# Five edits of a two-layer encoder trunk: unit setting, conv taps, V of the meta rows, input rows, last FFN part

## The chip, the cores and the metric

The kernel runs on one core of a Trainium2 chip. A core has TensorE (PE) for matrix products, VectorE (DVE), ScalarE (ACT) and GpSimd (POOL) for work on rows and elements, and SyncE (SP), which here starts most of the transfers. Each engine works through its own instructions in their order; semaphores tie the engines together. The metric is the device time of one execution in microseconds (us); the median of three runs of the kernel before is 1964.85.

## The reference, cut to what matters

The input is 512 tokens of width 1024; 16 learned meta rows are put in front, so 528 rows go through. A layer norm comes first, then two layers of the same form.

```
h = concatenate([meta, x]); h = layer_norm(h, ln_in_g, ln_in_b)
for l in range(2):
    h = layer_norm(ALPHA * h + 0.5 * swiglu_ffn(h, ffn1_w13[l], ffn1_w2[l]), ...)
    z = h @ w_in[l]                       # xp, ca, cg, q, k, v, g
    y_pool = trailing means of xp over 2, 4, 8, 16 rows, minus xp, times a matrix
    y_conv = silu(layer_norm(depthwise conv of ca * sigmoid(cg), 31 taps)) @ w_pw
    y_ret  = retention, 4 heads: rope(q), rope(k), chunk-causal decay, v, norm, silu gate
    h = layer_norm(ALPHA * h + concatenate([y_pool, y_conv, y_ret]) @ w_out[l], ...)
    h = layer_norm(ALPHA * h + 0.5 * swiglu_ffn(h, ffn2_w13[l], ffn2_w2[l]), ...)
return h[16:]
```

## The kernel before, in words

The activations lie with features on the 128 partitions and rows along the free dimension, in two halves of 264 rows (256 tokens and 8 meta rows). A product in float32 accuracy is made of three matmuls on rounded parts: high by high, high by low, low by high. The high part of a weight tile is a ScalarE cast, the low part a VectorE subtraction (`weights`, L86 to L95). Weight tiles rotate through small pools: 4 raw ones, 5 high and 5 low ones. Another pool, `wide`, has 16 tiles of 128 x 558 for rows of the mixers and for some splits. PSUM has four banks with the tag `acc`, two `att`, two `stat`.

The stages are the input (to about 66 us), an FFN, the mixer `m0` (about 366 to 610), two FFNs, the mixer `m1` (about 1335 to 1575), and the last FFN `f1b` (`last_ffn`), whose output leaves as rows of tokens.

A mixer computes the gated conv input u (two tiles `m1u`) and xp (`m1xp`), then V (L664 to L693): for each of four token tiles (`tt` 0 to 3) and the 16 meta rows (`tt` 4) a product of 24 matmuls of 512 columns, its means per head (VectorE, L684, L685) and the centred V (ScalarE, L690). Then follow, head by head, K and Q: a product (`m1kp`, `m1qp`, one `acc` bank each), a rotation (`rotary`, ScalarE copies L701 and L702, VectorE L703 to L705; `m1k00r` is K of head 0, half 0), for K a copy of the 8 rotated meta columns by GpSimd into `m1km` (L794), the scores (L719), the sums over V (L738) and the gate (`m1gp`).

Three kinds of work run beside this. The conv taps are 62 VectorE instructions over 128 x 528 (31 taps for two tiles `m1y`; the first of a tile is L608, the others L610). `PACE` says how many of them the program hands out per step of a head (L817 ff.). The window sums of the pooling are GpSimd copies and additions (L639, L642, tiles `m1sm` in `wide`), ScalarE copies (L641) and three VectorE rows (L645 to L647). The splits of the weights (L91, L94) are the third.

The program's order is not the engines' order: a scheduler places each instruction on its engine, and may put one that is written later into an earlier place where its operands and its tile are there.

The last FFN has five parts; in the last of them the output columns are taken in two halves (`ch`), in the first half by hidden unit over four token tiles, in the second by token tile. Then, tile by tile, `measure` and `root` make the norm's statistics, `scale` and `leave` apply them with the gain and bias rows and start the output transfers.

## Time and profile before

| what | value |
|---|---|
| median of three runs | 1964.85 us (1963.27, 1964.85, 1964.92) |
| the profiled execution | 1963.63 us, span 1961.8 us |
| busy: TensorE, VectorE, ScalarE, GpSimd | 1907.0, 1526.4, 909.2, 217.4 us |
| matmuls recorded | 14471 |

The span is the time from the first to the last instruction that the profiler saw; 1.8 us of the execution lie outside it. Busy time is read per stretch: a row of the table of stretches says how many of its microseconds an engine worked and at which clock TensorE ran (PEclk, 1.00 is 2.4 GHz and 0.50 is 1.2 GHz). In a timeline "x5" means that five instructions of the line were merged, and the brackets say how long the engine sat idle before the first one, and what it waited for.

### The profile page before, as it was taken

The numbers are of one execution on the slowest core, as the hardware profiler recorded it, in microseconds if no ns is written. First come the engines' busy times: TensorE is split into PE (matmuls) and PEld (weight loads), VectorE is DVE, ScalarE is ACT, GpSimd is POOL, SyncE is SP. The second block draws the span as 40 slices with busy tenths as digits, with TensorE's granted clock in tenths as the row PEclk, the third lists the DMA queues.
The fourth block names the chain that finished last, engine by engine and source line by source line (L and its number), as shares of the span: only waits on it lengthen the run. The fifth ranks groups of instructions, "written<-read, shape, count | busy, mean of one in ns | idle before, by whom it ended". The sixth has DMA issues, their size and how long they took to land.

```text
span 1961.8 us, 36780 instructions
## 1 busy us (share of the span) xinstructions
PE 1907.0 (97%) x14471; PEld 1824.0 (93%) x14471; DVE 1526.4 (78%) x3426; ACT 909.2 (46%) x1817; POOL 217.4 (11%) x283
## 2 busy tenths in 40 slices
PE   7999999999999999999999999999999999999996
PEld 6999999897899999999999999998889999999995
DVE  7788778689767887778696788787897686877787
ACT  5454446444333644455464454454343265544461
POOL 4000000442003000000120000005320130000001
PEclk9999999999999999999999999999999999999998
DMA  4422323322112223223223323332231213323321
GB/s 144 130 89 95 119 87 105 101 76 86 63 33 76 65 97 119 87 97 105 90 71 103 108 81 103 98 129 65 65 105 55 65 44 119 119 76 108 108 97 43
DMA packets 61068, 177.98 MB, mean 91 GB/s; under 512 B 6976, under 2 KB 10944, under 8 KB 60896
## 3 DMA queue, kind: packets, MB, share of 16 engines
q1 hardware_dynamic: 59744, 174.59, 27.9%
q8 instruction: 113, 1.85, 0.4%
q10 hardware_dynamic: 1152, 1.05, 0.2%
q14 instruction: 59, 0.48, 0.1%
HBM read 173.52 MB, written 2.10 MB: 90 GB/s over the span
## 4 chain that ended last, share of the span: by engine, by line
PE 82%; DVE 11%; issue 2%; ACT 2%; POOL 2%; DMA 0%; SPq 0%; DVEq 0%; POOLq 0%; ACTq 0%
PE f1bo L890 2%; PE f1bo L888 2%; PE f1bo L889 2%; PE f1a_y L134 2%; PE f0a_y L134 2%; PE f0b_y L134 2%; PE f1a_y L135 2%; PE f0b_y L133 2%; PE f0b_y L135 2%; PE f1a_y L133 2%; PE f0a_y L133 2%; PE f0a_y L135 2%; DVE m1y L610 1%; PE m1sc L719 1%; PE m0o L738 1%
## 5 line engine op out<-in xcount | busy, mean ns | idle before, releaser
L610 DVE SCALAR_TENSOR_TENSOR m1y<-m1u,vec,m1y 128x528 f32<-128x528 f32 x60 | 46.1, 803 | 0.0
L91 ACT CAST f0b_o_h<-f0b_o_r 128x512 fp32r<-128x512 f32 (+1 forms) x37 | 23.4, 636 | 48.7 <-PE f0b_y L134 29.6
L91 ACT CAST f0a_o_h<-f0a_o_r 128x512 fp32r<-128x512 f32 (+1 forms) x37 | 23.4, 635 | 48.6 <-PE f0a_y L134 29.5
L610 DVE SCALAR_TENSOR_TENSOR m0y<-m0u,vec,m0y 128x528 f32<-128x528 f32 x60 | 45.9, 801 | 0.0
L91 ACT CAST f1a_o_h<-f1a_o_r 128x512 fp32r<-128x512 f32 (+1 forms) x37 | 23.4, 636 | 48.4 <-PE f1a_y L134 29.6
L335 DVE TENSOR_TENSOR x<-x,f0a_y 128x264 f32<-128x264 f32 x64 | 27.2, 426 | 23.2 <-PE f0a_y L135 23.1
L335 DVE TENSOR_TENSOR h<-h,f1a_y 128x264 f32<-128x264 f32 x64 | 27.1, 425 | 23.1 <-PE f1a_y L135 23.0
L335 DVE TENSOR_TENSOR h<-h,f0b_y 128x264 f32<-128x264 f32 x64 | 27.1, 425 | 23.0 <-PE f0b_y L135 22.9
L94 DVE TENSOR_TENSOR f1bw_l<-f1bw_r,f1bw_h 128x512 fp32r<-128x512 f32 x42 | 27.7, 688 | 17.6 <-ACT f1bw_h L91 17.0
L949 POOL TENSOR_TENSOR yt<-yt,g_last 128x256 f32<-128x256 f32 x4 | 3.0, 739 | 333.2 <-ACT yt L948 333.2
L94 DVE TENSOR_TENSOR f0a_o_l<-f0a_o_r,f0a_o_h 128x512 fp32r<-128x512 f32 (+1 forms) x42 | 26.7, 642 | 13.8 <-ACT f0a_o_h L91 11.7
L94 DVE TENSOR_TENSOR f0b_o_l<-f0b_o_r,f0b_o_h 128x512 fp32r<-128x512 f32 (+1 forms) x42 | 26.6, 642 | 13.8 <-ACT f0b_o_h L91 11.7
L94 DVE TENSOR_TENSOR f1a_o_l<-f1a_o_r,f1a_o_h 128x512 fp32r<-128x512 f32 (+1 forms) x42 | 26.7, 642 | 13.7 <-ACT f1a_o_h L91 11.4
L278 POOL TENSOR_TENSOR f0b_ln_s<-h,h 128x264 f32<-128x264 f32 x2 | 1.6, 820 | 310.0 <-DVE h L335 310.0
L587 POOL MEMSET m0u<- 128x30 f32 x2 | 0.2, 123 | 304.0 <-PE f0a_20Q L135 304.0
L587 POOL MEMSET m1u<- 128x30 f32 x2 | 0.2, 123 | 303.1 <-PE f1a_20Q L135 303.1
L894 DVE TENSOR_TENSOR yt<-yt,f1bo 128x256 f32<-128x256 f32 x80 | 27.8, 415 | 5.4 <-PE f1bo L890 5.3
L91 ACT CAST f1bw_h<-f1bw_r 128x1024 fp32r<-128x1024 f32 (+1 forms) x22 | 22.1, 1011 | 21.1 <-PE f1bo L890 4.2
L291 ACT ACTIVATE m_ln_q<-h 128x264 f32<-128x264 f32 (+1 forms) x32 | 11.9, 414 | 39.7 <-DVE h L289 36.2
L257 PE MATMUL tr<-ident,xtok 128*128 128x128 f32 (+1 forms) x48 | 10.9, 328 | 11.9 <-DVE xtok L242 11.3
L257 PEld LDWEIGHTS tr<-ident,xtok 128*128 128x128 f32 (+1 forms) x48 | 6.8, 167 | 16.0 <-issue 14.7
L281 POOL TENSOR_TENSOR m_ln_s<-m_ln_s,h 128x264 f32<-128x264 f32 (+1 forms) x20 | 18.3, 914 | 30.8 <-DVE h L329 24.8
(10715 smaller groups left out, 9301.2 us busy)
## 6 DMA issues: line engine op xcount, KB each, us to landing
f1bw_r<-in_w2last SPq DMA_DIRECT2D x20, 512.0 KB, 3.9
f0a_o_r<-in_w SPq DMA_DIRECT2D x32, 256.0 KB, 2.7
f0b_o_r<-in_w SPq DMA_DIRECT2D x32, 256.0 KB, 2.8
f1a_o_r<-in_w SPq DMA_DIRECT2D x32, 256.0 KB, 2.8
m0wo_r<-in_w_out SPq DMA_DIRECT2D x8, 512.0 KB, 3.5
m1wo_r<-in_w_out SPq DMA_DIRECT2D x8, 512.0 KB, 3.5
m0w_r<-in_w_in SPq DMA_DIRECT2D x6, 512.0 KB, 4.0
m1w_r<-in_w_in SPq DMA_DIRECT2D x6, 512.0 KB, 4.2
```

The lines of the kernel that those rows point to most:

```text
L91: nc.scalar.copy(out=hi[:, :n], in_=w[:, :n])
L94: e.tensor_tensor(out=lo[:, sl], in0=w[:, sl], in1=raw(hi[:, sl]), op=ALU.subtract)
L133: nc.tensor.matmul(out, lhsT=wh, rhs=xh, start=start, stop=False, skip_group_check=onto)
L134: nc.tensor.matmul(out, lhsT=wh, rhs=xl, start=False, stop=False, skip_group_check=onto)
L135: nc.tensor.matmul(out, lhsT=wl, rhs=xh, start=False, stop=stop, skip_group_check=onto)
L335: nc.vector.tensor_tensor(out=y, in0=y, in1=ps, op=ALU.add)
L610: nc.vector.scalar_tensor_tensor(out=ys[c], in0=src, scalar=wk, in1=ys[c], op0=ALU.mult, op1=ALU.add)
L719: nc.tensor.matmul(sc[:kn, :cw], lhsT=kk[ks][:, kc : kc + kn], rhs=qq[s][:, c0 : c0 + cw], start=True, stop=True)
L888: nc.tensor.matmul(o, lhsT=hh, rhs=wh, start=part > 0 and i == 0, stop=False)
L889: nc.tensor.matmul(o, lhsT=hh, rhs=wl, start=False, stop=False)
L890: nc.tensor.matmul(o, lhsT=hl, rhs=wh, start=False, stop=i == nk - 1)
L894: nc.vector.tensor_tensor(out=y[:, :256], in0=y[:, :256], in1=o, op=ALU.add)
```

## The change

1. "Four plain units": the constant `PLAIN` is 4 in both files; no line of the diff touches it.
2. Taps: `PACE` is smaller, 28 taps are handed out ahead of the head loop (`EARLY`), and the others are tied by `issue_after` to the last rotation or gate.
3. V of the meta rows: one stationary tile of 48 columns holds the high parts (0 to 15), zeros, and the low parts (32 to 47). So two matmuls do what three did; the low part's rows are copied by ScalarE and added by VectorE in a new `wide` tile, `m1vm`.
4. Input: the meta rows are normalised by ScalarE instead of GpSimd, and first of their group.
5. The last part of the last FFN: its weights are all loaded ahead, and each token tile goes through both column halves, its statistics and its way out before the next one's products.

```diff
@@ -38,7 +38,7 @@
...
-PACE = (4, 3, 3, 2, 0)
+EARLY, PACE = 28, (1, 1, 2, 2, 0)
...
@@ -235,13 +235,11 @@
...
         for c in range(2):
-            for i, tt in enumerate(group):
+            for i, tt in reversed(list(enumerate(group))):
                 y = tok[tt][c]
                 p = y.shape[0]
                 if i == 0:
                     last = nc.vector.tensor_scalar(out=y, in0=y, scalar1=mv[:p, i, 0:1], scalar2=rs[:p, i : i + 1], op0=ALU.subtract, op1=ALU.mult)
-                elif i == 2:
-                    nc.gpsimd.tensor_scalar(out=y, in0=y, scalar1=mv[:p, i, 0:1], scalar2=rs[:p, i : i + 1], op0=ALU.subtract, op1=ALU.mult)
                 else:
                     nc.scalar.activation(y, y, AF.Identity, scale=rs[:p, i : i + 1], bias=nb[:p, i : i + 1])
         entered["last"] = last.ins
@@ -664,22 +662,33 @@
 
         xm = []
         for k in range(KT):
-            pair = sq_pool.tile([P, 2, NM], F32R, tag="xm", name=f"{name}xm{k}", bufs=KT)
+            pair = sq_pool.tile([P, 48], F32R, tag="xm", name=f"{name}xm{k}", bufs=KT)
+            nc.gpsimd.memset(raw(pair[:, NM:32]), 0.0)
             for p_ in range(2):
                 for s in range(2):
-                    nc.gpsimd.tensor_copy(pair[:, p_, s * HM : (s + 1) * HM], raw(xs[k][s][p_][:, 256:NT]))
-            xm.append((pair[:, 0, :], pair[:, 1, :]))
+                    nc.gpsimd.tensor_copy(pair[:, 32 * p_ + s * HM : 32 * p_ + (s + 1) * HM], raw(xs[k][s][p_][:, 256:NT]))
+            xm.append(pair)
...
         wv = [weights(a["w_v"][l, j], 1024, f"{name}wv{j}") for j in range(4)]
         for tt in range(5):
             n = NM if tt == 4 else P
             ps = acc(f"{name}v{tt}")
             for k in range(KT):
-                xh, xl = xm[k] if tt == 4 else at(xs[k][tt // 2], slice(tt % 2 * P, (tt % 2 + 1) * P))
                 wh, wl = at(wv[k // 2], slice((k % 2) * 512, (k % 2 + 1) * 512))
+                if tt == 4:
+
+                    nc.tensor.matmul(ps[:48], lhsT=xm[k], rhs=wh, start=k == 0, stop=False)
+                    nc.tensor.matmul(ps[:48], lhsT=xm[k], rhs=wl, start=False, stop=k == KT - 1)
+                    continue
+                xh, xl = at(xs[k][tt // 2], slice(tt % 2 * P, (tt % 2 + 1) * P))
                 nc.tensor.matmul(ps[:n], lhsT=xh, rhs=wh, start=k == 0, stop=False)
                 nc.tensor.matmul(ps[:n], lhsT=xh, rhs=wl, start=False, stop=False)
                 nc.tensor.matmul(ps[:n], lhsT=xl, rhs=wh, start=False, stop=k == KT - 1)
+            if tt == 4:
+                vm = wide(f"{name}vm")
+                nc.scalar.copy(out=vm[:n, :512], in_=ps[32 : 32 + n])
+                nc.vector.tensor_tensor(out=vm[:n, :512], in0=ps[:n], in1=vm[:n, :512], op=ALU.add)
+                ps = vm[:, :512]
...
             nc.vector.tensor_reduce(out=mu[:n], in_=ps[:n].rearrange("p (h e) -> p h e", h=HEADS), axis=mybir.AxisListType.X, op=ALU.add)
...
@@ -696,13 +705,15 @@
...
+        made = {}
+
...
-            nc.vector.tensor_tensor(out=r[:, :n], in0=r[:, :n], in1=r2[:, :n], op=ALU.add)
+            made["last"] = nc.vector.tensor_tensor(out=r[:, :n], in0=r[:, :n], in1=r2[:, :n], op=ALU.add).ins
...
@@ -765,7 +776,7 @@
...
-            nc.scalar.activation(g[:, : no[s]], ps[:, : no[s]], AF.Silu)
+            made["last"] = nc.scalar.activation(g[:, : no[s]], ps[:, : no[s]], AF.Silu).ins
...
@@ -809,6 +820,8 @@
...
+        for _ in range(EARLY):
+            next(taps)
...
@@ -816,10 +829,11 @@
             if hd < 2:
                 pool_y[hd] = pool_windows(hd)
             for i, _ in enumerate(work(hd, before)):
-                for _ in range(PACE[hd]):
-                    next(taps, None)
                 if hd == HEADS or i > 0:
                     next(steps, None)
+                with tc.issue_after(made["last"]):
+                    for _ in range(PACE[hd]):
+                        next(taps, None)
...
@@ -869,6 +883,8 @@
...
+            if part == len(PARTS) - 1:
+                break
...
@@ -894,25 +910,12 @@
...
-                if part == len(PARTS) - 1 and ch == 1:
-
-                    for tt in range(3):
-                        for i in steps:
-                            step(i, tt)
-                        for j in range(2):
-                            add(tt, j, ps[tt][:, j * 256 : (j + 1) * 256])
+                for i in steps:
+                    for tt in range(4):
+                        step(i, tt)
+                for tt in range(4):
...
-                        o = ps[3] if j == 0 else acc(f"{name}o{ch}4")
-                        for i in steps:
-                            step(i, 3, j * 256, 256, o[:, :256])
-                        add(3, j, o[:, :256])
-                else:
-                    for i in steps:
-                        for tt in range(4):
-                            step(i, tt)
-                    for tt in range(4):
-                        for j in range(2):
-                            add(tt, j, ps[tt][:, j * 256 : (j + 1) * 256])
+                        add(tt, j, ps[tt][:, j * 256 : (j + 1) * 256])
...
@@ -933,37 +936,55 @@
...
-                if tt == 1:
+                if tt < 3:
...
-            if tt == 1:
-                nb = sq_pool.tile([P, 3], F32, tag="nb", name=f"{name}nb", bufs=2)[:, :1]
+            if tt < 3:
+                nb = sq_pool.tile([P, 3], F32, tag="nb", name=f"{name}nb{tt}", bufs=2)[:, :1]
...
-                if tt == 1:
+                if tt < 3:
...
-                    nc.gpsimd.tensor_tensor(out=y, in0=y, in1=g_[j][:, :256], op=ALU.mult)
-                    nc.gpsimd.tensor_tensor(out=y, in0=y, in1=b_[j][:, :256], op=ALU.add)
-                elif (tt, j) in ((2, 1), (2, 3), (3, 3)):
+                    e = nc.gpsimd if tt < 2 else nc.vector
+                    e.tensor_tensor(out=y, in0=y, in1=g_[j][:, :256], op=ALU.mult)
+                    nc.vector.tensor_tensor(out=y, in0=y, in1=b_[j][:, :256], op=ALU.add)
+                elif j % 2:
...
+
+        c0 = done * 512
+        w_last = [[], []]
+        for i in range(0, nk, 2):
+            cw = min(2, nk - i) * 512
+            for ch, make in enumerate((weights, weights_wide)):
+                w = make(a["w2last"][ch, :, c0 + i * 512 : c0 + i * 512 + cw], cw, f"{name}l{ch}{i}")
+                w_last[ch] += w if ch else [at(w, slice(c, c + 512)) for c in range(0, cw, 512)]
...
+            ts = slice((tt % 2) * P, (tt % 2 + 1) * P)
+            for ch in range(2):
+                for c, cw in ((0, 256), (256, 256)) if (tt, ch) == (3, 1) else ((0, 512),):
+                    o = acc(f"{name}l{tt}{ch}{c}")
+                    for i in range(nk):
+                        wh, wl = (x[:, c : c + cw] for x in w_last[ch][i])
+                        hh, hl = at(hid[full[i]][tt // 2], ts)
+                        nc.tensor.matmul(o[:, :cw], lhsT=hh, rhs=wh, start=i == 0, stop=False)
+                        nc.tensor.matmul(o[:, :cw], lhsT=hh, rhs=wl, start=False, stop=False)
+                        nc.tensor.matmul(o[:, :cw], lhsT=hl, rhs=wh, start=False, stop=i == nk - 1)
+                    for k in range(0, cw, 256):
+                        y = yt[tt][2 * ch + (c + k) // 256]
+                        nc.vector.tensor_tensor(out=y[:, :256], in0=y[:, :256], in1=o[:, k : k + 256], op=ALU.add)
...
-            if tt == 3:
-                with tc.issue_after(met[tt]):
-                    leave(2)
...
-            if tt != 2:
-                leave(tt)
+            leave(tt)
...
```

Where the scheduler puts the instructions is seen in the order of the rows on each engine; three places are shown, of before and of the change apart.

VectorE in the second mixer, from V to the first rotation of K, before. `m1u` is the gated input of the convolution, `m1y` its result, `m1vmu` the means of V (the 16-row one belongs to the meta rows), the rows with `_l` are splits, `cosb` and `sinb` are the rotation's tables:

```order
L608 TENSOR_SCALAR m1y_17765<-m1u_17474,vec 128x528
L610 SCALAR_TENSOR_TENSOR m1y_17764<-m1u_17404,vec,m1y_17764 128x528
...
L94 TENSOR_TENSOR m1wq_l<-m1wq_r,m1wq_h 128x512 x2
L610 SCALAR_TENSOR_TENSOR m1y_17764<-m1u_17404,vec,m1y_17764 128x528
L94 TENSOR_TENSOR m1wk_l<-m1wk_r,m1wk_h 128x512 x2
L684 TENSOR_REDUCE m1vmu_17995<-m1v_17970 16x4
...
L610 SCALAR_TENSOR_TENSOR m1y_17765<-m1u_17474,vec,m1y_17765 128x528
L703 TENSOR_TENSOR m1k00r<-m1kp_0_18028,cosb 128x264
L704 TENSOR_TENSOR m1k00r_18054<-m1k00r_18054,sinb 128x264
L610 SCALAR_TENSOR_TENSOR m1y_17764<-m1u_17404,vec,m1y_17764 128x528
L705 TENSOR_TENSOR m1k00r<-m1k00r,m1k00r_18054 128x264
```

The same place in the changed kernel:

```order
L694 TENSOR_SCALAR m1vmu_17938<-m1vmu_17938 128x4
L693 TENSOR_REDUCE m1vmu_17972<-m1v_17947 128x4
L94 TENSOR_TENSOR m1wq_l<-m1wq_r,m1wq_h 128x512 x2
L94 TENSOR_TENSOR m1wk_l<-m1wk_r,m1wk_h 128x512 x2
L606 TENSOR_SCALAR m1y_17767<-m1u_17407,vec 128x528
L690 TENSOR_TENSOR m1vm<-m1v_17981,m1vm 16x512
L606 TENSOR_SCALAR m1y_17768<-m1u_17477,vec 128x528
L693 TENSOR_REDUCE m1vmu_18001<-m1vm 16x4
L608 SCALAR_TENSOR_TENSOR m1y_17767<-m1u_17407,vec,m1y_17767 128x528
...
L608 SCALAR_TENSOR_TENSOR m1y_17768<-m1u_17477,vec,m1y_17768 128x528
L643 TENSOR_TENSOR m1sm_2_18047<-m1sm_2_18047,inv_n 128x16
...
L714 TENSOR_TENSOR m1k00r<-m1kp_0_18062,cosb 128x264
```

The taps that stood among the means of V now all stand behind the splits and the meta sum; in the second piece the first dots are 25 more rows of L608 and one on the mean (L694), the others two rows of the window sums and nothing else. In the first mixer the rows stand in the same way.

ScalarE at the same place, before (`m1xp` is the pooling's input, `m1sm` a window sum, `m1vc` the centred V):

```order
L597 COPY m1xp_17537<-m1pxp_0_17674 128x8
L641 COPY m1sm_2_18013<-m1sm_1_18010 64x541
L597 COPY m1xp_17708<-m1pxp_0_17710 128x256
...
L641 COPY m1sm_8_18190<-m1sm_4_18187 64x535
L690 ACTIVATE m1vc_17862<-m1v_17834,m1vmu_17859 128x128 x2
...
L91 CAST m1wg_h<-m1wg_r 128x1024
L91 CAST m1wq_h<-m1wq_r 128x1024
L690 ACTIVATE m1vc_17998<-m1v_17970,m1vmu_17995 16x128 x2
...
L701 COPY m1k00r_18054<-m1kp_0_18028 64x264
```

And in the changed kernel:

```order
L595 COPY m1xp_17540<-m1pxp_0_17677 128x8
L595 COPY m1xp_17711<-m1pxp_0_17713 128x256
L595 COPY m1xp_17711<-m1pxp_0_17713 128x8
...
L91 CAST m1wg_h<-m1wg_r 128x1024
L689 COPY m1vm<-m1v_17981 16x512
L91 CAST m1wq_h<-m1wq_r 128x1024
L639 COPY m1sm_2_18047<-m1sm_1_18044 64x541
L712 COPY m1k00r_18088<-m1kp_0_18062 64x264
```

The copies of the window sums (`m1sm`) stood ahead of the centred V; the first of them now stands behind the copy of the meta rows (`m1vm`) and just ahead of the rotation's copies.

VectorE at the end, from the last addition of a product to the last row, before (`yt` are the output rows, four pieces of 256 columns per token tile; `f1brs` a statistic's root):

```order
L894 TENSOR_TENSOR yt_20874<-yt_20874,f1bo_24134 128x256
L210 BN_AGGR f1bmv_24243<-f1b_st 128x2
L938 SCALAR_TENSOR_TENSOR yt_20867<-yt_20867,f1bmv_24243,g_last_24151 128x256
...
L938 SCALAR_TENSOR_TENSOR yt_20870<-yt_20870,f1bmv_24243,g_last_24157 128x256
L938 SCALAR_TENSOR_TENSOR yt_20871<-yt_20871,f1bmv_24270,g_last_24151 128x256
...
L938 SCALAR_TENSOR_TENSOR yt_20874<-yt_20874,f1bmv_24270,g_last_24157 128x256
L955 SCALAR_TENSOR_TENSOR yt_20867<-yt_20867,f1brs_y,b_last_24159 128x256
...
L955 SCALAR_TENSOR_TENSOR yt_20871<-yt_20871,f1brs_y,b_last_24159 128x256
L955 SCALAR_TENSOR_TENSOR yt_20872<-yt_20872,f1brs_y,b_last_24161 128x256
L955 SCALAR_TENSOR_TENSOR yt_20873<-yt_20873,f1brs_y,b_last_24163 128x256
```

And in the changed kernel:

```order
L983 TENSOR_TENSOR yt_20880<-yt_20880,f1bl_24285 128x256
L954 TENSOR_TENSOR yt_20873<-yt_20873,b_last_23965 128x256
L953 TENSOR_TENSOR yt_20874<-yt_20874,g_last_23959 128x256
...
L209 BN_STATS f1b_st<-yt_20880 128x6
L954 TENSOR_TENSOR yt_20876<-yt_20876,b_last_23971 128x256
L210 BN_AGGR f1bmv_24302<-f1b_st 128x2
L941 SCALAR_TENSOR_TENSOR yt_20877<-yt_20877,f1bmv_24302,g_last_23957 128x256
...
L177 TENSOR_SCALAR f1brs_y<-f1brs_y 128x1
L959 SCALAR_TENSOR_TENSOR yt_20877<-yt_20877,f1brs_y,b_last_23965 128x256
L959 SCALAR_TENSOR_TENSOR yt_20879<-yt_20879,f1brs_y,b_last_23969 128x256
```

Before, three token tiles' scalings and roots are mixed behind the last addition, 46 rows in all; now the third tile's last rows and the fourth tile's own follow, 28 in all.

## Rows read from the trace of the kernel before

**Rows 1.** The page: busy time, share, instructions per engine.

```profile
PE 1907.0 (97%) x14471; PEld 1824.0 (93%) x14471; DVE 1526.4 (78%) x3426; ACT 909.2 (46%) x1817; POOL 217.4 (11%) x283
```

**Rows 2.** TensorE's waits: us in total, times, longest.

```profile
PE m1sc L719 <- POOL m1km L794: 3.5, 1, 3.5
PE m0sc L719 <- POOL m0km L794: 3.4, 1, 3.4
```

**Rows 3.** Table of stretches around the second mixer's first scores.

```profile
core 0: us, PE busy (x) PEld busy (x) DVE busy (x) ACT busy (x) POOL busy (x), PEclk, DMA share, GB/s
1421.60:1439.10 17.50, 17.50 (x145) 17.30 (x143) 17.50 (x34) 10.96 (x24) 6.19 (x2) 1.00 0.54 172
...
1442.60:1446.20 3.60, 3.55 (x14) 2.81 (x14) 3.60 (x9) 1.18 (x1) 1.62 (x1) 0.58 0.34 132
...
1450.00:1540.00 90.00, 90.00 (x614) 79.85 (x614) 70.91 (x235) 30.53 (x64) 3.35 (x6) 1.00 0.18 58
```

**Rows 4.** TensorE, second mixer: meta rows of V, K, first scores (durations: min/median/max).

```profile
L680 PE MATMUL m1v<-m1wv_h,m1xm x8: 389/393/397, 1416.1 to 1420.9; 128*16 128x512 f32 x8
...
L133 PE MATMUL m1kp<-f1a_ln_x0h,m1wk_h x8: 281/288/288, 1421.6 to 1496.0; 128*128 128x264 f32 x8
...
1442.65 0.60 PE L719 MATMUL m1sc<-m1q00r,m1km 128*16 128x256 f32 x2 [3.54 <-POOL m1km L794]
```

**Rows 5.** VectorE, same place, in order of time: start, us.

```profile
1391.21 0.54 DVE L608 TENSOR_SCALAR m1y<-m1u,vec 128x528 f32<-128x528 f32 x1
...
1394.04 5.17 DVE L610 SCALAR_TENSOR_TENSOR m1y<-m1u,vec,m1y 128x528 f32<-128x528 f32 x5
...
1401.22 4.55 DVE L610 SCALAR_TENSOR_TENSOR m1y<-m1u,vec,m1y 128x528 f32<-128x528 f32 x5
...
1412.63 4.15 DVE L610 SCALAR_TENSOR_TENSOR m1y<-m1u,vec,m1y 128x528 f32<-128x528 f32 x6
...
1426.04 1.28 DVE L94 TENSOR_TENSOR m1wk_l<-m1wk_r,m1wk_h 128x512 fp32r<-128x512 f32 x2
...
1431.00 0.41 DVE L703 TENSOR_TENSOR m1k00r<-m1kp,cosb 128x264 f32<-128x264 f32 x1
...
1432.37 0.41 DVE L705 TENSOR_TENSOR m1k00r<-m1k00r,m1k00r 128x264 f32<-128x264 f32 x1
```

**Rows 6.** ScalarE, same place.

```profile
1418.23 1.14 ACT L690 ACTIVATE m1vc<-m1v,m1vmu 128x128 f32<-128x128 f32 x4 [4.28 <-DVE m1vmu L685]
1419.25 1.07 ACT L91 CAST m1wq_h<-m1wq_r 128x1024 fp32r<-128x1024 f32 x1
```

**Rows 7.** GpSimd, same place: window sums, copies of the meta columns.

```profile
1395.36 1.09 POOL L642 TENSOR_TENSOR m1sm<-m1xp 128x542 f32<-128x542 f32 x1 [2.39 <-ACT m1xp L597]
...
1401.43 1.74 POOL L642 TENSOR_TENSOR m1sm<-m1sm 64x535 f32<-64x535 f32 x1
1432.91 3.75 POOL L794 COPY m1km<-m1k00r 128x8 f32<-128x8 f32 x1 [29.74 <-DVE m1k00r L705]
1436.60 6.00 POOL L794 COPY m1km<-m1k01r 128x8 f32<-128x8 f32 x1
```

**Rows 8.** VectorE, the second mixer's last tap.

```profile
1480.25 0.76 DVE L610 SCALAR_TENSOR_TENSOR m1y<-m1u,vec,m1y 128x528 f32<-128x528 f32 x1
```

**Rows 9.** TensorE's transposes at the input; ScalarE's rows of the same step.

```profile
13.03 2.10 PE L257 MATMUL tr<-ident,xtok 8*128 8x8 f32 x7 [0.68 <-POOL xtok L244]
...
L246 ACT ACTIVATE xtok<-xtok,in_nb,in_y x4: 800/807/816, 10.7 to 33.3; 128x512 f32<-128x512 f32 x4
```

**Rows 10.** The tail: TensorE's last matmul, VectorE scalings, its last rows.

```profile
1943.98 0.29 PE L890 MATMUL f1bo<-f1bw_h,f1b_20x_l 128*128 128x256 f32 x1
...
1946.99 0.49 DVE L938 SCALAR_TENSOR_TENSOR yt<-yt,f1bmv,g_last 128x256 f32<-128x256 f32 x1
...
1948.86 0.96 DVE L938 SCALAR_TENSOR_TENSOR yt<-yt,f1bmv,g_last 128x256 f32<-128x256 f32 x1
...
1956.79 1.74 DVE L955 SCALAR_TENSOR_TENSOR yt<-yt,f1brs_y,b_last 128x256 f32<-128x256 f32 x3
```

## The prediction

> **What bounds the kernel now.** I read the page's busy shares first, then the waits of TensorE, then a table of stretches of the second mixer, then the timelines of VectorE, GpSimd and ScalarE in the stretch where that mixer turns from V to the scores, and last the tail. TensorE is busy 97% of the span, VectorE 78% [rows 1]. So almost nothing is to be gained by hiding work; a change pays if it takes matmuls away, shortens a TensorE wait, or shortens what follows the last matmul. The waits are few: 3.5 and 3.4 us before the first scores of each mixer (TensorE waits for GpSimd's copy of the rotated meta columns, km) [rows 2] and 0.68 us at the input. Around the second mixer's wait VectorE is the full one: 17.50 of 17.50 us ahead of it and 3.60 of 3.60 us behind it [rows 3]. Behind 1450 TensorE has 90.00 of 90 us: whatever it loses in the head of a mixer is not won back. The profiled execution took 1963.63 us (span 1961.8); the median is 1964.85, 1.2 above, so I add 1.2 at the end.
>
> **Four plain units.** The constant that counts them stands unchanged in both kernels; this part does nothing. No term.
>
> **V of the meta rows, and the taps.** These meet in one place, the head of each mixer; I work it in the second one, whose times stand in the rows, and take the first as equal, since its wait is equal [rows 2].
> Removed: 8 of 24 matmuls of 512 columns. Twenty-four begin at 1416.1 and K's first product at 1421.6 [rows 4], 0.231 us each, so V now ends at 1416.1 + 16 x 0.231 = 1419.8, 1.8 us earlier.
> Moved: before, VectorE's taps fill the time of V. They run from 1391 on, some 30 before K's first product is there, and the rotation of K follows at 1431.00 [rows 5]. In the changed order only the means of V, the splits of q and k weights and the meta sum stand in V's time; all of the first 28 taps come behind the splits, 26 of them without a break, and the rotation of K stands behind them. VectorE is then idle during V, where nobody needs it, and full when the rotation is needed.
> When the block starts: in the changed order the second k cast stands behind the q cast and four rows on V; a cast is 1.07 us, the four rows 1.14 [rows 6]. Its weight buffer comes free within the meta product, as the meta product's first four matmuls free the q buffer (about 1417.0). So the cast ends about 1420.3, its split (1.28) at 1421.5, then two first taps (0.54 each), the meta sum and its mean (two rows over 512 columns, each about as half a split, 0.64): about 1424.0 [rows 5].
> How long it is: a tap takes 4.15/6 = 0.69 us where GpSimd is idle, but 1.03 and 0.91 where GpSimd's window sums run beside it (five in 5.17, five in 4.55) [rows 5, 7]. In the changed order ScalarE's share of the window sums stands behind the meta copy, so the sums now run beside the block. Bounds: 26 x 0.69 = 17.9 and 26 x 1.03 = 26.8. GpSimd's second chain, 1395.4 to 1403.2, cost those ten taps 1.7 + 1.1 = 2.8 us; the first chain is about half as long, 1.3 more. I take 17.9 + 4.1 = 22.0, nearest to the short end as GpSimd is done after some 11 us. The block ends at 1446.0 (1441.9 to 1450.8).
> What waits: K's second-head product uses the PSUM bank of its first (four banks, and four products K00, K01, Q00, Q01 stand between), so it must wait for the first rotation row. The four products take 96 x 0.121 = 11.6 us (145 matmuls in 17.50 us [rows 3]), to 1431.4. Three rows of the window sums (one over 512 columns, two of 16: 0.9 by the split's half) and the first rotation row (0.41) follow the block: TensorE resumes at 1447.3, idle for 16 us where it had no gap. Behind the waiting product stand the other K product, the scores, the gates: all of it is TensorE's path. The 48 matmuls last 5.8 us at 2.4 GHz. After the 3.54-us wait of before the granted clock was 0.58 of full over 3.6 us, so mostly 1.2 GHz, against 1.00 ahead of it [rows 3, 4]; I take the same slow stretch once, 7.4 us, to 1454.7 (10.3 if all are slow).
> The scores also need km. Rotated K00 is done about 1.1 us behind the first rotation row. Before, the two km copies ended 1442.60, 9.8 us behind the end of K00's rotation (1432.78), in 3.75 and 6.00 us [rows 5, 7]. That gives 1458.2 at the old pace; K01's rotation follows 2 us behind K00's, so the copies end 1451 or so at the earliest. The answer lies between 1454.7 (where TensorE gets there) and 1458.2. I take 1456.5: 13.8 us later than 1442.65. Bounds: 1441.9 + 1.3 + 5.8 = 1449.0, +6.4; 1450.8 + 2.4 + 9.8 = 1463.0, +20.4. V's shorter product is inside these, since they are ends.
> After it: the slow clock behind the old wait cost about 14 x 0.1 = 1.3 us; shorter waits may now save it: -0.5 (-1.3 to 0).
> Later in the mixer: 19 taps used to follow the first scores, now 29 do (28 plus five in order before): 10 x 0.69 = 6.9 us more on VectorE, which has 70.91 of 90 us [rows 3], so room on the whole. But the last tap moves from 1480.25 [rows 8] to the row just before the convolution's norm, in the changed order behind the last head's Q; its slack goes. Nothing if it still comes in time, up to about 5 us if the sums, mean and root follow late: +1.5 (0 to 5).
> A mixer: 13.8 - 0.5 + 1.5 = +14.8 (5 to 25); two: +29.6 (10 to 50).
>
> **Input.** GpSimd's meta rows held TensorE 0.68 us at 13.03; ScalarE's 128-row form of the same step takes 0.81 each [rows 9]. If ScalarE's four are done by then, -0.7; if its longer list delays the casts behind it, 0. I take -0.7 (-1 to +0.5).
>
> **Last part by token tiles.** The matmuls are equal in number and width, so no gain there; what changes is when tiles leave. Before, 17.5 us follow the last matmul (1943.98 + 0.3 to 1961.8): 46 rows on VectorE, some of them stretched from 0.49 to 0.96 (the scalings), the last one ending at 1958.5, and 3.3 us of output transfer [rows 10]. In the changed order 28 rows follow the last addition: 7 of tile 2 at about 0.36, statistics 0.5, four scalings at 0.4, eleven root steps of which the last nine follow each other at about 0.17, two last rows at 0.44: about 7.9 us, then ScalarE's product and GpSimd's sum of the last two pieces, in part behind each other, 1.5 by such rows of 0.48, and the same 3.3: 12.7. Gain 4.8. Against it: all six weight loads of the part must be split before tile 0 has both halves, and the wide buffers they go to come free only in the last hidden unit: 0 to 4 us of TensorE wait, I take 1.8. Net -3.0 (-8 to +2).
>
> **Sum.** 1963.6 + 29.6 - 3.0 - 0.7 = 1989.5, plus 1.2: **1991 us**.
>
> **Rivals.**
> (a) GpSimd gets no turn inside the block. For it: km copies of eight columns took 3.75 and 6.00 us under dense taps [rows 7]. Against it: the windows' rows of 1.1 to 1.7 us did get through between taps, and it was the taps that grew. Then the block ends at 1441.9; the first windows (3.5 us) hold the rows before the rotation to 1445.4, the second chain ends at 1453.2 and km, at half the old pace (5 us), at 1458.2: +15.6, with the later terms +16.6 per mixer, time 1994. By the Trainium skill, page "SBUF — State Buffer", section "Who interferes with whom", this is the case: a VectorE instruction with two SBUF inputs and a GpSimd one that reads SBUF exclude each other, and the second blocks until the first ends. The trace agrees with the exclusion in the copies' 3.75 and 6.00 us, but the window rows show turns being taken. Chance 0.17.
> (b) Everything slow: all 26 taps at 1.03, km at the old pace, the tail of the convolution late: +25 per mixer, 1963.6 + 50 - 3.7 + 1.2 = 2011. GpSimd has only 11 us of sums for the block, which speaks against. Chance 0.10.
> (c) Not slower: the taps run faster in a block with nothing between them. It decides at a rate: to have K's second head done by 1442.65 the block must end at 1442.65 - 5.8 - 1.3 = 1435.5, 11.5 us after its start, 0.44 us a tap. Then only gains remain: -2 x 1.3 - 3.0 - 0.7, 1958.5. For it: the one-input form of a tap takes 0.54 [rows 5]. Against: no stretch of two-input taps is under 0.69. Chance 0.07.
> (d) All bounds of the block on their good side and the tail at -8: 10 - 8 - 1, 1966, no change that could be told. Chance 0.06.
> The forecast has 0.60, its own range 1981 to 2001 (mixers 10 to 20 each). With a and most of b, 1974 to 2007 leaves out c, d and the upper end of b, about 0.2. What a measurement can tell here is 0.2%, 3.9 us: faster 0.07 (c), same 0.06 (d), slower 0.87.
>
> **What would show it.** In the changed profile: TensorE's longest wait is that of the second head's K product for VectorE's rotation row, about 16 us in each mixer, with a low granted clock behind it; VectorE idle for most of V and then 26 taps in a row, some 22 us; the wait for km shorter than 3.5 us or about that; V's meta product 3.7 us; the end 12 to 14 us behind the last matmul. If the wait for K's bank is missing or under 5 us, the forecast's main step is wrong, whatever the time. If the wait is there and the total is not over 1974, the time came back somewhere that I called full.

## The result and the profile after

The changed kernel takes 1994.23 us (median of four runs, 1992.61 to 1998.09) against 1964.61 for the kernel before on the same chip: a ratio of 1.0155, 95% interval 1.0137 to 1.0173, so 29.6 us slower. Its profiled execution took 1993.79 us, span 1992.0. Medians here and below are of fast executions: one execution of a later kernel (36 taps ahead) took 2523.59 us at a granted clock of 0.681 and is left out, with its profile. TensorE's waits say where to look: the two waits for km [rows 2] are gone, and others stand in their place.

The page's busy line, and TensorE's waits (us in total, times, longest):

```profile
PE 1912.9 (96%) x14455; PEld 1829.3 (92%) x14455; DVE 1524.0 (77%) x3431; ACT 917.0 (46%) x1832; POOL 200.8 (10%) x294
```

```profile
PE m0kp L133 <- DVE m0k00r L714: 13.6, 1, 13.6
...
PE m1kp L133 <- DVE m1k00r L714: 11.0, 1, 11.0
PE f0a_0p L134 <- POOL x_l L266: 2.9, 2, 2.2
PE m0gp L135 <- DVE m0wg_l L94: 2.6, 1, 2.6
```

TensorE's work fell by the 16 matmuls of V (14471 to 14455) and its busy time still rose by 5.9 us [rows 1]. The first mixer alone rises by 5.7 us from its K products on, where the matmuls behind the gap run at a lower granted clock (below).

Where the 30.2 us of span come from I read by stage: the first or last matmul of a stage's tile in the groups by tile, after against before, to 0.1 us.

| stage (what marks its end) | late by, us | added in it |
|---|---|---|
| input and first FFN (first mixer's first product) | +4.8 | +4.8 |
| first mixer to its first scores | +16.4 | +11.6 |
| first mixer, rest (first product of f0b) | +23.6 | +7.2 |
| two FFNs | +24.8 | +1.2 |
| second mixer to its first scores | +32.4 | +7.6 |
| second mixer, rest (first product of f1b) | +33.0 | +0.6 |
| last FFN to the last matmul | +32.7 | -0.3 |
| behind the last matmul | +30.2 | -2.5 |

So the first mixer costs 18.8, the second 8.2, the input 4.8, and the last part gives 2.8 back. Equal mixers, as I had taken them, are not what is there.

**Second mixer.** The table of stretches: the K and Q products, TensorE's gap, the products behind it, and 88 us of the rest of the mixer (against [rows 3]).

```profile
core 0: us, PE busy (x) PEld busy (x) DVE busy (x) ACT busy (x) POOL busy (x), PEclk, DMA share, GB/s
1444.60:1456.20 11.60, 11.60 (x97) 11.48 (x95) 11.32 (x19) 7.62 (x15) 0.00 (x0) 1.00 0.41 124
1456.20:1467.20 11.00, 0.10 (x1) 0.00 (x0) 11.00 (x20) 1.04 (x1) 0.00 (x0) 0.72 0.00 0
1467.20:1475.10 7.90, 7.85 (x48) 7.74 (x48) 7.90 (x21) 2.21 (x6) 1.95 (x2) 0.74 0.01 2
1482.00:1570.00 88.00, 87.47 (x611) 78.10 (x610) 78.91 (x243) 29.85 (x61) 3.08 (x6) 1.00 0.25 77
```

In the gap VectorE is full and TensorE idle; behind it 48 matmuls take 7.85 us at a mean granted clock of 0.74, between the two levels of 0.50 and 1.00 (1.2 and 2.4 GHz), against 5.8 us at 1.00 (half of the 11.60 us ahead of the gap). VectorE and GpSimd there, in order of time (against [rows 5, 7]):

```profile
1441.15 0.69 DVE L693 TENSOR_REDUCE m1vmu<-m1v 128x4 f32<-128x512 f32 x1 [4.68 <-PE m1v L686]
...
1448.22 0.75 DVE L608 SCALAR_TENSOR_TENSOR m1y<-m1u,vec,m1y 128x528 f32<-128x528 f32 x1
...
1448.96 17.05 DVE L608 SCALAR_TENSOR_TENSOR m1y<-m1u,vec,m1y 128x528 f32<-128x528 f32 x25
...
1466.78 0.41 DVE L714 TENSOR_TENSOR m1k00r<-m1kp,cosb 128x264 f32<-128x264 f32 x1
```

```profile
1414.25 1.25 POOL L640 TENSOR_TENSOR m1sm<-m1xp 128x542 f32<-128x542 f32 x1 [11.82 <-ACT m1xp L595]
...
1416.18 1.09 POOL L640 TENSOR_TENSOR m1sm<-m1sm 64x541 f32<-64x541 f32 x1
...
1424.67 1.33 POOL L640 TENSOR_TENSOR m1sm<-m1sm 64x535 f32<-64x535 f32 x1
1468.35 0.95 POOL L805 COPY m1km<-m1k00r 128x8 f32<-128x8 f32 x1 [42.34 <-DVE m1k00r L716]
1469.98 1.01 POOL L805 COPY m1km<-m1k01r 128x8 f32<-128x8 f32 x1 [0.68 <-DVE m1k01r L716]
```

VectorE waits 4.68 us for V's next tile where taps stood before [rows 5]. Then comes the block: one tap and, behind a short row, 25 more at 0.68 us each (17.05 / 25). The rotation row that TensorE waits for comes behind them. GpSimd's window sums are over by 1426, some 20 us ahead of the block, and the taps keep their pace.

**First mixer.** The same block, but GpSimd differs:

```profile
451.77 0.11 POOL L666 MEMSET m1xm<- 128x16 f32 x1 [39.26 <-PE m0v L681]
...
455.10 0.11 POOL L666 MEMSET m1xm<- 128x16 f32 x1 [0.42 <-PE m0v L681]
...
457.74 20.21 POOL L640 TENSOR_TENSOR m0sm<-m0sm 64x541 f32<-64x541 f32 x1
...
482.77 1.34 POOL L640 TENSOR_TENSOR m0sm<-m0sm 64x535 f32<-64x535 f32 x1
```

```profile
459.94 17.06 DVE L608 SCALAR_TENSOR_TENSOR m0y<-m0u,vec,m0y 128x528 f32<-128x528 f32 x25
477.99 0.17 DVE L643 TENSOR_TENSOR m0sm<-m0sm,inv_n 128x16 f32<-128x16 f32 x1 [0.99 <-POOL m0sm L640]
...
483.91 0.43 DVE L714 TENSOR_TENSOR m0k01r<-m0kp,cosb 128x264 f32<-128x264 f32 x1 [2.56 <-ACT m0k01r L713]
```

The tiles of the meta rows (`xm`) are shared by both mixers. The eight zero-fills for the second mixer's tiles therefore wait on TensorE until the first mixer's V has read them, and GpSimd, which works in order, holds the first mixer's window sums behind them for 39 us. The sums then meet the block, and one that takes 1.09 us in the second mixer (1416.18 above, the same shape) lasts 20.21 us. Behind it, VectorE's rotation has small waits. TensorE waits 2.6 us more for a split of the gate's weights, and its granted clock in that stretch is 0.61:

```profile
489.30:500.00 10.70, 8.05 (x28) 5.97 (x29) 8.35 (x20) 1.62 (x5) 0.86 (x2) 0.61 0.07 10
```

**Input.** ScalarE and GpSimd; first two rows of before, one of each engine, then the changed kernel:

```profile
12.12 1.03 ACT L91 CAST f0a_0u_h<-f0a_0u_r 128x1024 fp32r<-128x1024 f32 x1
...
22.35 0.75 POOL L268 TENSOR_TENSOR x_l<-x,x_h 128x264 fp32r<-128x264 f32 x1 [0.54 <-ACT x_h L266]
```

```profile
11.31 2.93 ACT L244 ACTIVATE xtok<-xtok,in_nb,in_y 8x512 f32<-8x512 f32 x4
...
19.49 1.03 ACT L91 CAST f0a_0u_h<-f0a_0u_r 128x1024 fp32r<-128x1024 f32 x1
...
32.15 0.39 ACT L393 ACTIVATE f0a_0g<-f0a_0p 128x264 f32<-128x264 f32 x1 [5.92 <-PE f0a_0p L135]
```

```profile
20.60 1.29 POOL L94 TENSOR_TENSOR f0a_0u_l<-f0a_0u_r,f0a_0u_h 128x512 fp32r<-128x512 f32 x1 [3.48 <-ACT f0a_0u_h L91]
...
28.09 2.76 POOL L94 TENSOR_TENSOR f0a_21w_l<-f0a_21w_r,f0a_21w_h 128x512 fp32r<-128x512 f32 x2
30.80 0.74 POOL L266 TENSOR_TENSOR x_l<-x,x_h 128x264 fp32r<-128x264 f32 x1
```

The cast of the first FFN's second weight tile (`f0a_0u`) started at 12.12 us before; now it starts at 19.49, behind the four meta rows and the copies of x. GpSimd, which makes its low part, sits idle for 3.48 us until then, and splits of the next two weight tiles come ahead of its last low part of x. That one comes at 30.80, where 22.35 was before, and TensorE waits for it: 2.9 us in its two waits for the low parts, of the 4.8 by which the stage is late. For the other 1.9 no wait of that size is shown.

### The profile page after: what moved, and what is told of

The parts are those of the page before. It is cut to its first block, busy times and chain, and to the rows that moved or that the text cites. A ratio compares the mean times of both kernels' runs of the same rounds, so it can differ in the third digit from the quotient of the medians.

```text
span 1992.0 us, 36765 instructions
## 1 busy us (share of the span) xinstructions
PE 1912.9 (96%) x14455; PEld 1829.3 (92%) x14455; DVE 1524.0 (77%) x3431; ACT 917.0 (46%) x1832; POOL 200.8 (10%) x294
## 4 chain that ended last, share of the span: by engine, by line
PE 66%; issue 16%; DVE 9%; ACT 3%; POOL 3%; DMA 0%; POOLq 0%; ACTq 0%; DVEq 0%
PE f0b_y L134 2%; PE f0b_y L133 2%; PE f0a_y L134 2%; PE f0b_y L135 2%; PE f1a_y L134 2%; PE f0a_y L133 2%; PE f0a_y L135 2%; PE f1a_y L135 2%; PE f1a_y L133 2%; POOL m0sm L640 1%; DVE m1y L608 1%; PE m0o L749 1%; PE m0sc L730 1%; PE m1sc L730 1%; PE m1o L749 1%
## 5 line engine op out<-in xcount | busy, mean ns | idle before, releaser
L91 ACT CAST f1a_o_h<-f1a_o_r 128x512 fp32r<-128x512 f32 (+1 forms) x37 | 23.4, 635 | 48.5 <-PE f1a_y L134 29.6
L608 DVE SCALAR_TENSOR_TENSOR m0y<-m0u,vec,m0y 128x528 f32<-128x528 f32 x60 | 43.1, 755 | 0.0
L608 DVE SCALAR_TENSOR_TENSOR m1y<-m1u,vec,m1y 128x528 f32<-128x528 f32 x60 | 43.0, 755 | 0.0
L94 DVE TENSOR_TENSOR f0a_o_l<-f0a_o_r,f0a_o_h 128x512 fp32r<-128x512 f32 (+1 forms) x42 | 26.7, 643 | 13.8 <-ACT f0a_o_h L91 11.8
L94 DVE TENSOR_TENSOR f1a_o_l<-f1a_o_r,f1a_o_h 128x512 fp32r<-128x512 f32 (+1 forms) x42 | 26.6, 642 | 13.8 <-ACT f1a_o_h L91 11.5
L94 DVE TENSOR_TENSOR f1bw_l<-f1bw_r,f1bw_h 128x512 fp32r<-128x512 f32 x32 | 20.9, 688 | 9.5 <-ACT f1bw_h L91 9.2
L640 POOL TENSOR_TENSOR m0sm<-m0sm 64x541 f32<-64x541 f32 (+3 forms) x4 | 23.7, 5930 | 0.2
L255 PE MATMUL tr<-ident,xtok 128*128 128x128 f32 (+1 forms) x48 | 11.1, 329 | 11.8 <-DVE xtok L242 11.2
L91 ACT CAST f1bw_h<-f1bw_r 128x1024 fp32r<-128x1024 f32 x16 | 16.7, 1050 | 12.4 <-PE f1b_6Q L134 1.8
L910 DVE TENSOR_TENSOR yt<-yt,f1bo 128x256 f32<-128x256 f32 x64 | 21.9, 414 | 0.0
```

The source lines that it names most:

```text
L91: nc.scalar.copy(out=hi[:, :n], in_=w[:, :n])
L94: e.tensor_tensor(out=lo[:, sl], in0=w[:, sl], in1=raw(hi[:, sl]), op=ALU.subtract)
L255: nc.tensor.transpose(out=ps[:, c0 : c0 + p], in_=y[m // 4][:, m % 4 * P : (m % 4 + 1) * P], identity=ident[:p, :p])
L608: nc.vector.scalar_tensor_tensor(out=ys[c], in0=src, scalar=wk, in1=ys[c], op0=ALU.mult, op1=ALU.add)
L640: nc.gpsimd.tensor_tensor(out=dst[b:, w_:], in0=cur[b:, w_:], in1=cur[b:, : W - w_], op=ALU.add)
L910: nc.vector.tensor_tensor(out=y[:, :256], in0=y[:, :256], in1=o, op=ALU.add)
```

## The experiments

Each ran beside the kernel before on its own chip; ratios are against that one, and a time set against a kernel of another chip holds to about 1 us (the kernel before took 1964.06 to 1965.3 in the four groups of runs). Twelve kernels, first the meta sum, then the taps, the zero-fills, the input, the last part, and the joined repairs.

**The meta rows of V alone, as the change has them.** Before, with that hunk of the diff only (PACE as before); its last lines hold the sum:

```diff
...
+                vm = wide(f"{name}vm")
+                nc.scalar.copy(out=vm[:n, :512], in_=ps[32 : 32 + n])
+                nc.vector.tensor_tensor(out=vm[:n, :512], in0=ps[:n], in1=vm[:n, :512], op=ALU.add)
+                ps = vm[:, :512]
```

> The kernel before with the meta part of V alone, its sum in a tile of wide as in the changed kernel; the taps at the old pace and not tied. In this order no tap stands in V either: all 62 follow the first rotations, two to four between two of them. Theory (what costs is that VectorE stands idle in V and has the taps later; the block of 26 is the worst form of it, not the only one): TensorE waits less for the first rotation than in the changed kernel (under 3 us), but some 45 taps instead of 19 fall behind the first scores, 18 us more on VectorE where it has 19 us free, so waits all over the heads: +3 to +10 us a mixer, 1968 to 1984 us. Rival (only the unbroken block costs): V is shorter by 1.8 us a mixer and the rest fits, 1958 to 1964 us.

Measured 1987.0 us, ratio 1.0112 (1.0095 to 1.013): the theory's kind, above its range, and the rival falls. First the waits, then VectorE in the second mixer:

```profile
PE m0sc L730 <- DVE m0sm L741: 12.7, 3, 10.1
PE m1sc L730 <- DVE m1sm L741: 12.2, 3, 8.4
```

```profile
1424.21 0.69 DVE L695 TENSOR_REDUCE m1vmu<-m1v 128x4 f32<-128x512 f32 x1 [4.67 <-PE m1v L688]
...
1430.35 0.53 DVE L608 TENSOR_SCALAR m1y<-m1u,vec 128x528 f32<-128x528 f32 x1
```

The first tap starts at 1430.35, behind V, where it stood at 1391.21 before [rows 5], although no line on the taps was touched: the wide sum alone empties VectorE of taps during V. At the old pace the taps then fall between the rotations and the products with the decay (L741), and TensorE's next scores wait for these; the loss comes by another wait than in the changed kernel.

**The same with the sum in the PSUM bank**, through two small tiles and no `wide` one (the lines against the run above):

```diff
-                vm = wide(f"{name}vm")
...
+                for c in range(0, 512, 256):
+                    vm = t(f"{name}vm{c}", "q")
+                    nc.scalar.copy(out=vm[:n, :256], in_=ps[32 : 32 + n, c : c + 256])
+                    nc.vector.tensor_tensor(out=ps[:n, c : c + 256], in0=ps[:n, c : c + 256], in1=vm[:n, :256], op=ALU.add)
```

> The kernel before with the meta part of V alone, summed in PSUM without a wide tile; the old taps among the means of V. Theory (VectorE, full from 1400 to 1450, sets the time of the first scores, so eight matmuls less only lengthen TensorE's wait for km): the wait grows from 3.4 to about 5 us and the total falls by 0 to 1 us, 1963 to 1964.5 us. Rival (V's product is on TensorE's path and its 2 x 1.8 us come through): 1960 to 1961 us.

Measured 1964.53 us, ratio 0.9996 (0.9986 to 1.0005). Same arithmetic, same matmuls, 22 us apart: what costs is the sum in the `wide` tile. The runs do not part the tile from the place of the sum (SBUF or the PSUM bank). Why it moves the taps is not shown either. `m1y` asks for its tiles ahead of `m1vm` in the program of the changed kernel (L598, L688) but is first written behind it. In the trace of that kernel its first tap starts at 1446.09, 0.3 us behind the start of ScalarE's copy into `m1vm`, and ScalarE's copies of the window sums follow that copy. That the pool hands out its tiles in the order of first writing would fit; it is not shown. The theory's time came (1963 to 1964.5, at its upper end), though not by a longer wait for km. The 1.8 us that V became shorter bring nothing here, since the scores now wait 2.8 and 2.7 us for VectorE:

```profile
PE m0sc L730 <- DVE m0sm L741: 2.8, 1, 2.8
PE m1sc L730 <- DVE m1sm L741: 2.7, 1, 2.7
```

**The taps alone.** Before, with `EARLY`, the smaller `PACE` and `issue_after`:

> The kernel before with the taps' part alone: 28 ahead, the others tied, smaller pace. Theory (the taps' part is harmless or good by itself, the harm comes from where the joined kernel has room for them): the first scores of each mixer no longer wait 3.4 us for km, nor run at the low clock behind it, so 2 x (3.4 to 4.7): 1955 to 1958 us. Rival (the taps left over hold up the rest of the mixer): the gain is eaten by waits before the convolution's norm, 1963 us or more.

Measured 1960.09 us, ratio 0.9982 (0.9973 to 0.9991). This lies between the theory and the rival. With no wide sum the 28 taps stand in V's time, and the waits for km [rows 2] are gone. Part is given back: the second mixer's first scores come 4.2 us early, its end 2.0.

**The whole change, sum in the PSUM bank** (the edit as above):

> The changed kernel, but the low rows of the meta product are copied to two small tiles of another tag and added in the PSUM bank itself, so that the product takes no tile of the pool wide. In this order 28 taps stand among the means of V, ahead of the rotation of K. Theory (the block of taps behind V stands there because of that one wide tile): TensorE's waits of 13.6 and 11.0 us for the rotation go, and the wait for km is under 1 us, since no dense taps hold GpSimd; input +4.5 and last part -2.8 stay as in the changed kernel, the two mixers come out 4 to 6 us each faster than before: 1953 to 1960 us. Rival (the smaller pace of the taps is what costs, since few are left for the time of V and the convolution comes late): the waits move to the convolution's norm and the total stays over 1975 us.

Measured 1958.59 us, ratio 0.9978 (0.9968 to 0.9987): 35 us under the changed kernel by moving one sum. TensorE's two waits for the rotation row are gone, and taps are back in V:

```profile
1393.36 13.33 DVE L608 SCALAR_TENSOR_TENSOR m1y<-m1u,vec,m1y 128x528 f32<-128x528 f32 x13
```

```profile
1393.56 1.51 POOL L640 TENSOR_TENSOR m1sm<-m1sm 64x541 f32<-64x541 f32 x1
```

Here taps and sums do share: 13 taps at 1.03 us, the sum of the shape that was held for 20.21 us takes 1.51.

**The zero-fills on VectorE**, all else as changed:

```diff
-            nc.gpsimd.memset(raw(pair[:, NM:32]), 0.0)
+            nc.vector.memset(raw(pair[:, NM:32]), 0.0)
```

> The changed kernel with the eight zeroings of the meta tile on VectorE instead of GpSimd; the block of taps stays. Theory (in the first mixer GpSimd's queue holds the second mixer's zeroings, which wait for the first mixer's meta product, ahead of the window sums; these then meet the block, and one of them was held for 20.2 us): the window sums of the first mixer run during V as in the second, its wait for the rotation falls from 13.6 to about 11 us and the copies behind it come at once, 4 to 8 us: 1986 to 1990 us. Rival (the first mixer's window sums stand late for another reason, the wide tile): 1993 to 1995 us.

Measured 1983.77 us, ratio 1.0089 (1.0074 to 1.0104), some 10 us under the changed kernel (10.5 by the times; the first mixer of its profile is 9.9 shorter). Both mixers now wait alike, and the held sum is a short one, far ahead of the block:

```profile
PE m1kp L133 <- DVE m1k00r L714: 10.9, 1, 10.9
PE m0kp L133 <- DVE m0k00r L714: 10.9, 1, 10.9
```

```profile
426.49 1.08 POOL L640 TENSOR_TENSOR m0sm<-m0sm 64x541 f32<-64x541 f32 x1
```

The first mixer costs 8.9 us here instead of 18.8. It moved more than the theory gave: the 2.6-us wait for the gate's split went too, and the granted clock is 1.00 there.

**The input alone**, and, without the first pair of these lines, the same with the meta rows in their old place, last of the group, but on ScalarE:

```diff
-            for i, tt in enumerate(group):
+            for i, tt in reversed(list(enumerate(group))):
...
-                elif i == 2:
-                    nc.gpsimd.tensor_scalar(out=y, in0=y, scalar1=mv[:p, i, 0:1], scalar2=rs[:p, i : i + 1], op0=ALU.subtract, op1=ALU.mult)
```

> Before, with the input part alone (meta rows first, on ScalarE). Theory: ScalarE's four meta rows of 2.93 us in all stand ahead of its cast of the first weights, which ends some 7 us later, so TensorE's first product waits: the first block of the first part ends about 4.8 us later than before, and the whole is 4 to 5 us slower, about 1969. Rival: the loss shows only together with the other parts; then the time is that of before within 2 us. The prediction's own term, 0.7 us faster, stands as the third.

> Before, with the meta rows on ScalarE but in their old place, last of the four tiles. If the place in the row costs (meta rows ahead of the cast of the first weights), this one is within 1 us of before, or up to 0.7 us faster by the GpSimd wait that goes. If the engine costs (ScalarE has four more rows in the input), it is 3 to 5 us slower as well.

Measured 1969.9 us, ratio 1.0032 (1.0019 to 1.0044), and without the new order 1968.8, 1.0024 (1.0015 to 1.0033). So it is the engine that costs; what the place in the row adds cannot be told from zero. On ScalarE in the second of them:

```profile
10.51 2.93 ACT L244 ACTIVATE xtok<-xtok,in_nb,in_y 128x512 f32<-128x512 f32 x4
...
17.94 1.04 ACT L91 CAST f0a_0u_h<-f0a_0u_r 128x1024 fp32r<-128x1024 f32 x1
```

The four rows take 2.93 us, but the cast starts 5.8 us later than the 12.12 of before: with ScalarE's list longer, the schedule puts it behind all four copies of x.

**The whole change with the old input:**

> The changed kernel with the input's meta rows on GpSimd again and in the old order, all else as changed. Theory (ScalarE's four rows of 0.73 us push the casts behind them, and GpSimd's low parts of x fall behind the splits of the first weights): the 4.5 us that the transposes and the first products were late go, 1989 to 1991 us. Rival (the late start is absorbed by the first FFN, where transfers or casts were late anyway): 1993 to 1995 us.

Measured 1989.5 us, ratio 1.0132 (1.0117 to 1.0147), 4.7 less than the changed kernel; the two block waits stand at 13.6 and 11.0 as in the changed kernel. The input's cost is its own and adds up.

**The last part alone:**

> The kernel before with the last part by token tiles alone. Theory (the tail's gain is that of VectorE's shorter queue, 17.5 to 15.0 us, and the products are not delayed): 2.5 to 3 us, 1961.5 to 1962.2 us. Rival (part of it was given by the later start of that part in the changed kernel, so that loads were further ahead): 1963.5 us or more.

Measured 1962.65 us, ratio 0.999 (0.998 to 1.0). A small gain, not told apart from none by itself. In its profile the stretch behind the last matmul is 2.6 us shorter, as in the changed kernel, but 2.0 us were lost ahead of it, nearly all between the first mixer's scores and the second mixer's V, in stages that the edit does not touch.

**Both repairs:** the whole change with the sum in the PSUM bank and the old input.

> The changed kernel with both repairs, the meta sum in PSUM and the old input. Both theories: the two gains add, 1994 less 4.7 for the input and 35.6 for the mixers: 1953 to 1955 us. Rival (the input's late start had covered something in the first mixer): 1957 us or more.

Measured 1953.51 us, ratio 0.9937 (0.9922 to 0.9952), the fastest of all, 11.8 us under its kernel before. V, the end of V and the first heads' products, to the first scores, have no gap:

```profile
1389.00:1416.00 27.00, 27.00 (x122) 20.92 (x122) 24.94 (x40) 8.41 (x23) 8.72 (x9) 1.00 0.10 33
1416.00:1433.00 17.00, 17.00 (x143) 16.86 (x142) 16.28 (x34) 9.55 (x21) 1.74 (x3) 1.00 0.64 202
```

It gains more than its parts alone (-4.0 taps, -0.8 V, -1.4 last part). By stage the mixers give 4.6 and 5.6 here, and 2.0 and 2.2 with the taps alone: the shorter V, 1.8 each, counts once the taps no longer hold up the scores, and 0.8 and 1.6 stay without an account.

**More taps ahead**, on top of both repairs: 40 with `PACE` (1, 1, 1, 1, 0), and 36 with (1, 1, 2, 2, 0).

> The kernel with both repairs (sum in the PSUM bank, old input), with 40 taps ahead of the rotation at one to a row and none behind the last kind, where it had 28 at up to two. Theory: what it gives back behind the first scores comes from VectorE's later taps, which make the convolution's norm late; 12 taps at 0.69 us, 8 us less behind the scores, give back the 1 to 2 us that each mixer lost there: 1949 to 1953. Rival: V's time is full on VectorE (24.94 of 27 us busy), so 12 more taps push the rotation past K's bank and TensorE waits up to 8 us a mixer: 1955 to 1970, with the wait of the second head's K product for the rotation row back in the profile.

> As the run with 40 taps early, with 36, at up to two to a row. Theory: 1950 to 1954, no wait for K's bank. Rival (V's time is full): a wait of up to 5 us a mixer, 1955 to 1963, less than with 40.

Measured 1961.47 us, ratio 0.9986 (0.9977 to 0.9995), and 1957.49, 0.9966 (0.9954 to 0.9978). My theory fell: more taps ahead are slower, 28 is better than 36 and 36 than 40. The rival had the kind (V's time is full on VectorE) but not the place. With 40, it is the split of k's weights that comes late, not the rotation row; for 36 this is not shown:

```profile
PE m1kp L135 <- DVE m1wk_l L94: 3.2, 1, 3.2
PE m0kp L135 <- DVE m0wk_l L94: 3.2, 1, 3.2
```

## Why the prediction came out as it did

The total was right (1991 for 1994.23) and its main step too, the wait for K's rotation behind a block of taps. That it came within 3 us is in good part luck, since the terms that made it up were off and cancelled: forecast 14.8 and 14.8 for the mixers, -0.7 for the input and -3.0 for the last part; measured 18.8, 8.2, +4.8 and -2.8. The mixers together came out 2.6 under, the input 5.5 over.

*The wait in K's second head.* It is there, for VectorE's rotation row, with VectorE idle in V and a low clock behind it, as forecast: 13.6 and 11.0 us where I had 16. Its cause is the sum in the wide tile: the wait goes when the sum leaves it (1958.59), and the two runs of the meta rows alone are 22 us apart; the pacing of the taps by itself gains. The prediction took the changed order as the joint work of the two parts and did not ask which.

*The block, 22.0 us.* Failed by the 4.1 us for sums beside it: "the sums now run beside the block". In the second mixer GpSimd had done them in V, and 26 taps took 17.8 us (0.75 and 17.05), the short bound of 17.9. Only ScalarE's two copies of the windows stood behind the meta copy, and each is the end of its chain, which no sum of GpSimd reads.

*km.* Failed: "at the old pace" of 9.8 us. The two copies took 0.95 and 1.01 us instead of 3.75 and 6.00, and TensorE does not wait for them. The old prices were no property of the copy; before, VectorE was full beside it [rows 3], with taps, rotation rows and splits by turns. Together with the block this is what made 13.8 us into 7.6 in the second mixer. Its parts there: wait 11.0 for 3.5, products 2.0 slower, V 1.8 shorter, 7.7 in all.

*The slow stretch behind the gap.* Forecast 7.4 us for 48 matmuls, measured 7.85.

*Later in the mixer, +1.5.* 0.6 in the second; in the first 7.2, with the gate's split 2.6 us late and a second stretch at a low clock (0.61).

*Rival (a), GpSimd without a turn.* Its time, 1994, is the measured one, but by another sum. Its mechanism is what the first mixer shows, 20.21 us for one sum, and the zero-fills ahead of it, which I had not seen waiting, are why it met the block there. Moving them gave some 10 us back. The Trainium skill, page "SBUF — State Buffer", section "Who interferes with whom", has it that a VectorE instruction with two SBUF inputs and a GpSimd one reading SBUF exclude each other until the first is done. The 20.21 us agree with an exclusion, but it was 25 taps that went ahead of the sum and not one. That taps and sums took turns in V (1.03 and 1.51 us) agrees with the exclusion too, but not with one side going short; what decides between the two was not tried.

*Input, -0.7.* Failed, in sign. I counted the GpSimd wait that goes and bounded the delay of the casts at +0.5. I did not follow the cast of `f0a_0u`, 7.4 us later, on to GpSimd, which splits that tile: four splits of the next two weight tiles there come ahead of the last low part of x.

*Last part, -3.0.* The size is right (-2.8) by luck, its halves are not: TensorE loses nothing (-0.3 for +1.8), so the weight loads ahead of the part were hidden, and the tail gives 2.5 for 4.8. Span end minus last matmul, with its own 0.28 us: 15.0 where 17.5 was [rows 10] and 12.7 was forecast. The forecast counted from the last addition on VectorE and put nothing between the last matmul and that row:

```profile
1980.44 0.41 DVE L983 TENSOR_TENSOR yt<-yt,f1bl 128x256 f32<-128x256 f32 x1
```

It ends 3.8 us behind the last matmul (1977.02), since rows of the third tile's root and gain and of the fourth's statistics stand ahead of it. What follows it takes 11.1 us.

*V, 1.8 us.* Measured 1.8 in each mixer, but worth nothing by itself (1964.53).

*Rival (c), not slower.* It needed 0.44 us a tap; they took 0.68. Rivals (b) and (d) did not come.

## What to carry to other kernels

A temporary that takes a tile from a shared pool can cost far more than its instructions, when other users of the pool move behind it in the schedule (here the taps, 22 us): look at where the neighbours of the pool went before pricing the edit. When a piece of work goes to another engine, follow that engine's next operations to who waits for them, rather than its added time. On an engine that works in order, a clearing of a buffer for the next stage waits for the buffer's last reader and stops all that stands behind it. And a tail is counted from the last matmul, with the rows that a scheduler may have put ahead of its result.

## What the runs showed of the hardware

A GpSimd addition (64 x 541) lasted 20.21 us while VectorE ran 25 two-input taps without a break at 0.68 us each, their undisturbed pace; in another run the same two kinds, side by side, took turns, at 1.51 and 1.03 us. One-input copies of 128 x 8 by GpSimd (`km`) took from 0.19 to 6.00 us: 3.75 and 6.00 before, where VectorE was full [rows 3, 7], 0.95 and 1.01 just behind the block, 0.19 for the copy from `m1k11r` in the changed kernel. In a gap of 11.0 us with hardly a matmul TensorE's mean granted clock was 0.72; it was 0.74 over the next 7.90 us and 1.00 from 1482 to 1570.
